# Attention scores two steps earlier in a twelve-step head loop, and another spread of the filling

## The chip, the cores and the metric

The kernel runs on one core of a Trainium2 chip. The core has five engines that run side by side, each through its own queue of instructions: TensorE (PE) multiplies matrices, VectorE (DVE) and ScalarE (ACT) work elementwise, GpSimd (POOL) and SyncE (SP) are used here almost only to issue DMA transfers. The metric is the time of one execution on the device in microseconds (us); lower is better. Before the change it is 2144.18 us, the median of 3 runs (2140.3 to 2147.97).

## The reference

One decoder layer in float32 on 512 tokens of width 2048: RMSNorm, a token mixer, a residual add, RMSNorm, a SwiGLU feed-forward network, a residual add, a final RMSNorm. The mixer is sparse attention with three branches; with 512 tokens the selected and the window branch both see every earlier token, so that each head has two causal softmaxes over 512 keys and one over 31 compressed keys:

```python
def masked_softmax(s, mask):
    s = jnp.where(mask, s.astype(jnp.float32), NEG_INF)
    p = jax.nn.softmax(s, axis=-1)
    return jnp.where(mask, p, 0.0)
...
s_c = jnp.einsum('btghd,bcgd->bghtc', q, kcc) + bias_c
p_c = masked_softmax(s_c, mask_c)
...
o = (gates[:, :, 0, :, :, None] * o_c + gates[:, :, 1, :, :, None] * o_s
     + gates[:, :, 2, :, :, None] * o_w)
return o.reshape(Bsz, S, N_HEADS * DH) @ w_out
```

There are 16 heads of width 128 in 4 groups; a group shares its keys and values. Queries, keys, values and gates are slices of one product of the normed input with `nsa_w_in`.

## The kernel before

**Three products for one.** Every float32 operand is split into a high part and a rest: ACT copies the value to the shorter format (`hi`), DVE subtracts (`lo`). `three` (L267 to L269) then multiplies hi by hi, hi by lo and lo by hi. For a weight block of 128x1024 that is one ACT copy `whi` (L97) and one DVE subtraction `wlo` (L98), in `Weights.split`. `Weights.take` hands out the next block and splits the one three places further on; `load` fetches raw blocks into three buffers.

**The stage that the change touches** lies between about 200 and 715 us of the span: the attention of the 16 heads, written out by hand in one order for all engines (`manual_schedule`). Each engine executes its share in the order of the program text. Two kinds of work are woven together:

- *The filling* (`dense`, L728): 13 projections of later heads (units `qpair`, `kpair`, `vpair`, 32 groups of matmuls each, four weight blocks each, so a block is taken at every eighth group) and then four `partial` products with `nsa_w_out` (24 groups, three blocks each). A group counts 650 in `done["ns"]`. At the end of a unit its result leaves PSUM (`q_out`, `k_out`: on DVE `yt`, L319, then on ACT `qh`, L292, then on DVE `ql`, L293).
- *A head* in twelve steps: `scores(h, t)` for the token tiles t = 3, 2, 1, 0 (PE writes the one PSUM tile `s`; DVE adds the bias and takes the row extreme, three L797 instructions into `cx` and `u`; ACT exponentiates, L799), `finish(h, t)` (DVE scales and transposes `p`, L804 to L812, and SP stores it to `d_p` in four DMAs, L814), `fetch(t)` (SP loads it back in the turned layout into `ptr`, L818, after the stores have landed), `turn(h, b, kt)` (ACT copies `pth`, L835, DVE subtracts `ptl`, L839) and `values(h, b, kt)` (PE multiplies into the tile `o`; L850 for the compressed branch, b = -1). `head_out` (L855) lets ACT copy `o` to `stage` and SP store it.

While head h is turned and multiplied, the scores of head h + 1 are made. In the loop of head h, `turn` number i stands at step i (0 to 8) and `values` two steps later; `scores(h + 1, t)` stand at steps 2, 5, 8, 11, `finish(h + 1, t)` at steps 3, 6, 9 and at step 0 of the next loop; `fetch(3)` and `fetch(2)` at step 8, `fetch(1)` and `fetch(0)` at steps 0 and 3 of the next loop. Ahead of loop 0 the scores of head 0 are made. Each step ends with `pump(h, step)`, which issues filling until `done["ns"]` has reached a goal four steps ahead of the step: 20800 (one unit) for a head, so 32 groups in twelve steps. A weight block is thus taken, and one split, at the ends of steps 0, 3, 6 and 7 in the loops 2 to 11 (at step 7 the end of a unit draws the last split forward). `drain_to` is a safeguard that issues filling until a needed unit is done.

In unit 13 (`qpair(14)`, the filling of loops 11 and 12) the buffers of the normed input are free piece by piece: `reload_o(i)` (POOL, 1 MB) brings the outputs of heads 4i to 4i + 3 back, and `split_o(k)` (L699 on ACT, L700 on DVE, 128x1024 each) splits two heads for the `partial` products.

Of the kernel before, what the change touches and what calls it, by code (L numbers as in the profile page):

```python
# [19 lines left out]
S, D, H, DH, G, HPG = 512, 2048, 16, 128, 4, 4  # L20
# [153 lines left out]
def nsa_block(ctx: ExitStack, tc: tile.TileContext, x, rel_bias, mix_g, ffn_g, fin_g, w_in, w_out,  # L174
# [30 lines left out]
    def tok(t):  # L205
        return slice(128 * t, 128 * (t + 1))
# [59 lines left out]
    def three(o, ah, al, bh, bl, start, stop):  # L266
        mm(o, ah, bh, start=start, stop=False, skip_group_check=True)  # L267
        mm(o, ah, bl, start=False, stop=False, skip_group_check=True)  # L268
        mm(o, al, bh, start=False, stop=stop, skip_group_check=True)  # L269

    def ws(ps, gi, g, c0=0, c1=S, start=None, end=None, of=None):

        for u in range(2):
            cs = slice(128 * u, 128 * (u + 1))
            if end and gi == 3 and u:
                W.ahead(3)
            for k in range(4):
                kk = 4 * gi + k
                st = (kk == 0) if start is None else (start and kk == 0)
                three(ps[u][:, c0:c1], g[0][:, k, cs], g[1][:, k, cs],  # L280
                      *(x[:, kk, c0:c1] for x in of or (hn_h, hn_l)), st, kk == KC - 1)
                if end and gi == 3 and k == 3:
                    end(u)
                yield 650
# [57 lines left out]
    def q_out(ps, h0):  # L342
        def end(u):
            Q[h0 + u] = tuple(qp.tile([128, S], F32R, name=f"q{n}") for n in "hl")
            split_from(normed(ps[u], SCALE), Q[h0 + u][0], Q[h0 + u][1])

        return end
# [282 lines left out]
    with ExitStack() as st2:  # L630
# [18 lines left out]
        def proj2():  # L649
            pool_ = (psx, ps2)[next(units) % 2]  # L650
            return [pool_.tile([128, 512], F32, name="proj") for _ in range(2)]

        def qpair(h0):
            ps = proj2()
            end = q_out(ps, h0)
            for i in range(4):
                yield from ws(ps, i, W.take(), end=end)
                if h0 == H - 2 and i < 3:
                    reload_o(i)
                if h0 == H - 2 and i > 1:  # L660
                    split_o(i - 2)
            done["n"] += 1
            yield None

# [29 lines left out]
        def reload_o(i):  # L694
            pool.dma_start(hn_l[:, 4 * i:4 * i + 4].bitcast(F32), d_o[i].rearrange("h p s -> p h s"))

        def split_o(k):
            h, l = (x[:, 2 * k:2 * k + 2] for x in (hn_h, hn_l))
            act(h, l.bitcast(F32), AF.Copy)  # L699
            dve.tensor_tensor(l, l.bitcast(F32), h.bitcast(F32), op=OP.subtract)  # L700
# [39 lines left out]
        STEPS = 12  # L740

        def pump(h, step):
            at = h + (step + 4) / STEPS
            goal = 20800 * min(at, 13) + 22500 * max(at - 13, 0)
            while done["ns"] < goal:
                c = next(stream, "end")
                if c == "end":
                    return
                done["ns"] += c or 0

        def drain_to(n):
            while done["n"] < n:
                c = next(stream, "end")
                if c == "end":
                    return
                done["ns"] += c or 0

        def needed(h):

            return 4 * ((h - 2) // 4) + (1 if h % 4 > 1 else 3) if h > 1 else 0  # L760
# [4 lines left out]
        def load_bias(h):  # L765
            if h < H:
                TB[h] = ap_.tile([128, S], F32, name="tb")
                (nc.sync if h else pool).dma_start(TB[h], bass.AP(tensor=d_u.tensor, offset=d_u.offset + h * UL + 127,
                                                 ap=[[H * UL - 1, 128], [1, S]]))

        def branch(t, b):

            return P[t][:, :, 32 * (t + 1) * b:32 * (t + 1) * (b + 1)]

        def scores(h, t):
            g, n = h // HPG, 128 * (t + 1)
            (qh, ql), (kh, kl) = Q[h], KK[g % 2]
            if t == NT - 1:
                HS[h] = dict(
                    mx=ap_.tile([128, NT, 3], F32, name="mx"), sm=ap_.tile([128, NT, 3], F32, name="sm"))  # L780
            s = HS[h]
            at = 224 + (512 if t == 1 else 0)
            cuts = [0, 288] + [c for c in (800, 1056) if c <= 32 + 2 * n]
            if cuts[-1] < 32 + 2 * n:
                cuts.append(32 + 2 * n)
            for c0, c1 in zip(cuts, cuts[1:]):
                three(sc[:, at + c0:at + c1], qh[:, tok(t)], ql[:, tok(t)], kh[:, c0:c1], kl[:, c0:c1], True, True)
            c = CX[t][:, :NCMP]
            regions = [(c, c, c, sc[:, at:at + NCMP], biasc[:, h, 24 - 8 * t:24 - 8 * t + NCMP])]
            bt = TB[h][:, S - n:].rearrange("p (n s) -> p n s", s=128)  # L790
            sw = sc[:, at + 32:at + 32 + 2 * n].rearrange("p (n b s) -> p b n s", b=2, s=128)
            for b in range(2):
                u = ap_.tile([128, S], F32, name="u")[:, :n]
                regions.append((u.rearrange("p (n s) -> p n s", s=128), u.rearrange("p (n j s) -> p j n s", j=4, s=32),
                                branch(t, b).rearrange("p j (n s) -> p j n s", s=32), sw[:, b], bt))
            for i, (u, v, p, ps, bias) in enumerate(regions):
                dve.tensor_tensor_reduce(out=u, in0=ps, in1=bias, op0=OP.add, op1=OP.min, scale=-1.0,  # L797
                                         scalar=1e38, accum_out=s["mx"][:, t, i:i + 1])
                act(p, v, AF.Exp, bias=s["mx"][:, t, i:i + 1], scale=-1.0, accum_out=s["sm"][:, t, i:i + 1])  # L799
            s[t] = [c] + [branch(t, b) for b in range(2)]  # L800

        def finish(h, t):
            r = HS[h]["sm"][:, t]
            dve.reciprocal(r, r)  # L804
            dve.tensor_mul(r, r, gates[:, t, h])
            for i, p in enumerate(HS[h].pop(t)):
                o = p
                if not i:
                    o = P[t][:, :3, runs[t] - 32:]
                    p = CX[t].unsqueeze(1).to_broadcast([128, 3, 32])  # L810
                dve.tensor_scalar(o, p, r[:, i:i + 1], None, op0=OP.mult)
            dve.transpose(P[t], P[t])  # L812
            for i in range(4):
                nc.sync.dma_start(d_p[t][:, :, i].rearrange("j a r -> a j r"), P[t][32 * i:32 * (i + 1)])  # L814

        def fetch(t):

            nc.sync.dma_start(PT[:, :, PT_STEP * t:PT_STEP * t + runs[t]], d_p[t].rearrange("j a i r -> (j a) i r"))  # L818
# [47 lines left out]
        load_bias(0)  # L866
        load_bias(1)
        for i in range(4):
            scores(0, 3 - i)
            if i > 1:  # L870
                fetch(5 - i)
            if i:
                finish(0, 4 - i)
            pump(-1, min(9 + i, 11.7))
        for h in range(H):
            seq = [(b, kt) for kt in (3, 2, 1, 0) for b in (0, 1)] + [(-1, 0)]
            for i in range(STEPS):
                if i == 4:
                    load_bias(h + 2)
                if i in (0, 3):  # L880
                    fetch(1 - i // 3)
                if i < 9:
                    turn(h, *seq[i])
                if i == 8 and h + 1 < H:
                    fetch(3)
                    fetch(2)
                if i == 0:
                    finish(h, 0)
                if h + 1 < H:
                    if i == 2:  # L890
                        drain_to(needed(h + 1))
                    if i % 3 == 2:
                        scores(h + 1, 3 - i // 3)
                    elif i % 3 == 0 and i:
                        finish(h + 1, 4 - i // 3)
                if 2 <= i < 10 or i == 11:
                    if i == 2 and h % HPG == 0:
                        drain_to(h)
                    values(h, *seq[min(i - 2, 8)])
                    if i == 11:  # L900
                        head_out(h)
                pump(h, i)
# [592 lines left out]
```

## Time and profile before

| | |
|---|---|
| median of 3 runs | 2144.18 us |
| the profiled execution | 2143.05 us, of which 2141.3 us are the span of the page |
| PE busy | 2105.8 us (98%), 14697 matmuls |
| DVE busy | 1634.8 us (76%) |
| ACT busy | 929.2 us (43%) |
| granted TensorE clock, mean | 0.993 |

The share of PE is counted with modelled ends: a matmul counts as busy until the next one can follow, so short waits hardly show. In rows of the timeline the columns are start, duration (both in us), engine, line, operation, result<-operands, shapes, and in brackets how long the engine had stood idle before and for whom. In rows of windows they are the stretch, its length, and for PE, PEld, DVE, ACT and POOL the busy time with the number of instructions, then the granted clock, the share of the DMA engines and GB/s.

### The profile page before, as it was taken

To read this page: it belongs to the slowest core of one execution; us is meant where nothing else is said; L and a number is where in the kernel's file an instruction comes from. 1 tells how busy PE (TensorE), PEld (TensorE's weight loads), DVE (VectorE), ACT (ScalarE), POOL (GpSimd) and SP (SyncE) were. 2 spreads that over 40 slices of the span, in tenths; PEclk is the share of its full clock that TensorE was granted. 3 is DMA by queue.
4 is the path that set the end of the run, shared out by engine and by line. 5 is a ranking of instruction groups with operands and counts; after the bars stand their busy time and mean duration, and the time that the engine had idled before them with its cause. 6 is when DMAs were issued, how large, how long until landed. Compare 5 with 4: busy or idle time off the path is not lost.

```text
span 2141.3 us, 37148 instructions
## 1 busy us (share of the span) xinstructions
PE 2105.8 (98%) x14697; PEld 1951.4 (91%) x14697; DVE 1634.8 (76%) x2674; ACT 929.2 (43%) x1439; POOL 128.0 (6%) x209
## 2 busy tenths in 40 slices
PE   9999999999979999999999999999999999999998
PEld 7898788898969889899999999999999888989996
DVE  5565777877767347898888888888888787877785
ACT  5344455555544234434434344344344444544344
POOL 1000111111101000000000000000000000001000
PEclk9999999999989999999999999999999999999999
DMA  7554666666757633344434344343443776878894
GB/s 232 179 148 147 186 197 197 183 197 188 217 179 233 221 127 128 109 137 130 127 120 126 122 129 129 119 128 119 129 128 126 253 277 217 295 272 309 307 331 151
DMA packets 271867, 388.08 MB, mean 181 GB/s; under 512 B 34523, under 2 KB 204555, under 8 KB 271052
## 3 DMA queue, kind: packets, MB, share of 16 engines
q1 hardware_dynamic: 245932, 275.52, 41.0%
q0 software_dynamic: 23856, 105.98, 14.2%
q10 hardware_dynamic: 1904, 4.20, 0.5%
q8 instruction: 115, 1.88, 0.4%
q14 instruction: 60, 0.49, 0.1%
HBM read 320.52 MB, written 70.36 MB: 183 GB/s over the span
## 4 chain that ended last, share of the span: by engine, by line
PE 67%; DMA 1%; DVE 1%; ACT 1%; issue 0%; SPq 0%; ACTq 0%; DVEq 0%
PE f L268 19%; PE f L269 19%; PE f L267 19%; PE proj L267 1%; PE proj L268 1%; PE proj L269 1%; PE pp L267 1%; PE pp L268 1%; PE pp L269 1%; PE po L268 1%; PE po L267 1%; PE po L269 1%; DMA tt<-d_a 0%; PE pp L245 0%; DMA d_p<-p 0%
## 5 line engine op out<-in xcount | busy, mean ns | idle before, releaser
L98 DVE TENSOR_TENSOR wlo<-raw,whi 128x1024 fp32r<-128x1024 f32 (+1 forms) x226 | 270.7, 1200 | 115.2 <-ACT whi L97 115.1
L97 ACT ACTIVATE whi<-raw 128x1024 fp32r<-128x1024 f32 (+1 forms) x226 | 234.4, 1040 | 223.2 <-DVE raw L994 121.7
L994 DVE TENSOR_TENSOR tlo<-tt,thi 128x1536 fp32r<-128x1536 f32 (+2 forms) x135 | 197.1, 1460 | 109.7 <-ACT thi L1096 88.8
L267 PE MATMUL f<-hn_h,whi 128*128 128x256 f32 x984 | 271.7, 276 | 0.8 <-ACT E L1054 0.8
L269 PE MATMUL f<-hn_h,wlo 128*128 128x256 f32 x984 | 271.6, 276 | 0.0
L268 PE MATMUL f<-hn_l,whi 128*128 128x256 f32 x984 | 271.6, 276 | 0.0
L1091 ACT ACTIVATE whi<-raw 128x1024 fp32r<-128x1024 f32 x123 | 126.1, 1057 | 292.2 <-DVE raw L994 282.0
L267 PE MATMUL proj<-hn_h,whi 128*128 128x512 f32 x512 | 205.4, 401 | 0.5 <-ACT hn_h L402 0.5
L268 PE MATMUL proj<-hn_l,whi 128*128 128x512 f32 x512 | 201.7, 394 | 0.3 <-DVE hn_l L403 0.3
L269 PE MATMUL proj<-hn_h,wlo 128*128 128x512 f32 x512 | 201.6, 394 | 0.0
L267 PEld LDWEIGHTS f<-hn_h,whi 128*128 128x128 f32 x984 | 184.7, 188 | 1.2 <-ACT E L1054 1.2
L269 PEld LDWEIGHTS f<-hn_h,wlo 128*128 128x128 f32 x984 | 184.7, 188 | 0.0
L268 PEld LDWEIGHTS f<-hn_l,whi 128*128 128x128 f32 x984 | 184.7, 188 | 0.0
L1096 ACT ACTIVATE thi<-tt 128x1536 fp32r<-128x1536 f32 x82 | 121.9, 1487 | 84.1 <-PE f L268 84.1
L267 PE MATMUL proj<-whi,hn_h 128*128 128x256 f32 (+2 forms) x496 | 146.6, 296 | 5.9 <-ACT hn_h L699 5.9
L269 PE MATMUL proj<-whi,hn_l 128*128 128x256 f32 (+2 forms) x496 | 146.0, 294 | 2.1 <-DVE hn_l L700 2.1
L994 DVE TENSOR_TENSOR wlo<-raw,whi 128x1024 fp32r<-128x1024 f32 x123 | 147.0, 1223 | 0.0
L268 PE MATMUL proj<-wlo,hn_h 128*128 128x256 f32 (+2 forms) x496 | 145.5, 293 | 0.0
L269 PE MATMUL f<-whi,tlo 128*128 128x512 f32 x320 | 124.9, 390 | 0.6 <-DVE tlo L994 0.6
L268 PE MATMUL f<-wlo,thi 128*128 128x512 f32 x320 | 125.0, 391 | 0.3 <-DVE wlo L98 0.3
L267 PE MATMUL f<-whi,thi 128*128 128x512 f32 x320 | 124.7, 390 | 0.0
L839 DVE TENSOR_TENSOR ptl<-ptr,pth 128x128 fp32r<-128x128 f32 (+3 forms) x128 | 60.0, 485 | 76.7 <-ACT pth L835 72.9
(327 smaller groups left out, 6142.6 us busy)
## 6 DMA issues: line engine op xcount, KB each, us to landing
raw<-in_ffn_w_in SPq DMA_DIRECT2D x135, 512.0 KB, 3.6
raw<-in_ffn_w_out SPq DMA_DIRECT2D x88, 512.0 KB, 5.9
rawx<-in_ffn_w_in SPq DMA_DIRECT2D x41, 512.0 KB, 4.9
rawx<-d_a SPq DMA_DIRECT2D x31, 512.0 KB, 4.9
ah<-d_s POOLq DMA_DIRECT2D x16, 896.0 KB, 7.4
al<-d_s POOLq DMA_DIRECT2D x16, 896.0 KB, 10.1
raw<-in_nsa_w_in SPq DMA_DIRECT2D x24, 512.0 KB, 4.6
raw<-in_nsa_w_in POOLq DMA_DIRECT2D x24, 512.0 KB, 4.4
```

The lines of the kernel that those rows point to most:

```text
L97: self.nc.scalar.activation(hi[:, :n], src, AF.Copy)
L98: self.nc.vector.tensor_tensor(lo[:, :n], src, hi[:, :n].bitcast(F32), op=OP.subtract)
L267: mm(o, ah, bh, start=start, stop=False, skip_group_check=True)
L268: mm(o, ah, bl, start=False, stop=False, skip_group_check=True)
L269: mm(o, al, bh, start=False, stop=stop, skip_group_check=True)
L839: dve.tensor_tensor(tl4, src, th4.bitcast(F32), op=OP.subtract)
L994: dve.tensor_tensor(o, a, b, op=OP.subtract)
L1091: act(h, r, AF.Copy)
L1096: act(h, ttf, AF.Copy)
```

## The change

Four things are moved; no arithmetic is added or taken away.

1. `scores(h + 1, t)` stand at steps 0, 3, 6, 9 and `finish(h + 1, t)` at steps 1, 4, 7, 10: two steps earlier, counted in steps of the loop. `fetch(1)` stands at step 9 and `fetch(0)` at step 0 of the next loop, three steps earlier; `fetch(3)` and `fetch(2)` stay at step 8.
2. `pump` aims 4 + (4 - 2 at) steps ahead while `at`, the place in heads, is below 2: about nine steps ahead of loop 0, eight at its start, six at the start of loop 1, four from loop 2 on. The filling ahead of loop 0 is put before each of its scores, not after.
3. The last tile of head 0 is finished ahead of loop 0.
4. In `qpair(14)` each `reload_o` comes one quarter of the unit later, and `split_o(0)` and `split_o(1)` stand together at its end.

```diff
@@ qpair
-                if h0 == H - 2 and i < 3:
-                    reload_o(i)
-                if h0 == H - 2 and i > 1:
-                    split_o(i - 2)
+                if h0 == H - 2 and i:
+                    reload_o(i - 1)
+                    if i == 3:
+                        split_o(0)
+                        split_o(1)
@@ pump
-            at = h + (step + 4) / STEPS
+            at = h + step / STEPS
+            at += (4 + max(4 - 2 * at, 0)) / STEPS
@@ ahead of the loop of heads
         for i in range(4):
+            pump(-1, 5 + 2 * i)
             scores(0, 3 - i)
             if i > 1:
                 fetch(5 - i)
             if i:
                 finish(0, 4 - i)
-            pump(-1, min(9 + i, 11.7))
+        pump(-1, 11.7)
+        fetch(1)
+        finish(0, 0)
@@ the loop of heads
-                if i in (0, 3):
-                    fetch(1 - i // 3)
+                if i == 0:
+                    fetch(0)
                 if i < 9:
                     turn(h, *seq[i])
-                if i == 8 and h + 1 < H:
+                if i == 8 and more:
                     fetch(3)
                     fetch(2)
-                if i == 0:
-                    finish(h, 0)
-                if h + 1 < H:
-                    if i == 2:
+                if i == 9 and more:
+                    fetch(1)
+                if more:
+                    if i == 0:
                         drain_to(needed(h + 1))
-                    if i % 3 == 2:
+                    if i % 3 == 0:
                         scores(h + 1, 3 - i // 3)
-                    elif i % 3 == 0 and i:
-                        finish(h + 1, 4 - i // 3)
+                    elif i % 3 == 1:
+                        finish(h + 1, 3 - i // 3)
```

`more` is `h + 1 < H`. The order in which each engine gets its instructions follows from the text. In the loops 2 to 11 (one with a q unit as the example) DVE goes:

```
before: scores3, ptl, finish3, wlo, ptl, ptl, scores2, ptl, finish2, wlo, ptl, yt, ql, wlo, pth, scores1, yt, ql, finish1, scores0, ptl, finish0, wlo, ptl, ptl
after:  scores3, wlo, ptl, finish3, ptl, ptl, scores2, wlo, ptl, finish2, ptl, ptl, scores1, wlo, ptl, finish1, yt, ql, wlo, pth, yt, ql, scores0, finish0, ptl
```

(`scores3` is short for the three L797 instructions of t = 3, `finish3` for L804 to L812, `pth` for the subtraction of the compressed branch.) ACT has the matching copies and exponentials in the same order.

More of the change, by code (lines that the diff above doesn't have):

```diff
@@ L877, in nsa_block @@
             for i in range(STEPS):
+                more = h + 1 < H
                 if i == 4:
                     load_bias(h + 2)
-                if i in (0, 3):
-                    fetch(1 - i // 3)
+                if i == 0:
+                    fetch(0)
                 if i < 9:
                     turn(h, *seq[i])
-                if i == 8 and h + 1 < H:
+                if i == 8 and more:
                     fetch(3)
                     fetch(2)
-                if i == 0:
-                    finish(h, 0)
-                if h + 1 < H:
-                    if i == 2:
+                if i == 9 and more:
+                    fetch(1)
+                if more:
+                    if i == 0:
                         drain_to(needed(h + 1))
-                    if i % 3 == 2:
+                    if i % 3 == 0:
                         scores(h + 1, 3 - i // 3)
-                    elif i % 3 == 0 and i:
-                        finish(h + 1, 4 - i // 3)
+                    elif i % 3 == 1:
+                        finish(h + 1, 3 - i // 3)
                 if 2 <= i < 10 or i == 11:
```

## The prediction

> **What bounds the kernel now.** I first cut the heads' stage into windows: the start with loop 0, two steady loops, the place where the outputs are reloaded, the end.
>
> ```profile
> 201.78:254.73 52.95, 47.09 (x212) 38.77 (x212) 36.85 (x112) 22.82 (x67) 4.50 (x6) 0.94 0.60 171
> 494.33:524.19 29.86, 29.86 (x146) 25.06 (x145) 23.46 (x67) 15.44 (x43) 4.48 (x6) 1.00 0.70 198
> 524.19:554.06 29.87, 29.87 (x188) 26.88 (x187) 23.47 (x66) 15.22 (x41) 4.47 (x6) 1.00 0.68 196
> 594.00:626.00 32.00, 19.42 (x83) 16.04 (x82) 18.76 (x40) 12.60 (x25) 2.99 (x4) 0.73 0.66 202
> 706.00:713.00 7.00, 5.27 (x26) 3.36 (x25) 4.86 (x7) 1.67 (x3) 1.47 (x2) 1.00 0.34 108
> ```
>
> PE is idle for 5.9 us at the start (52.95 - 47.09), 12.6 us around 610 and 1.7 us at the end; the clock is lower in the first two. That is what the change can win. In the steady loops PE shows no idle time in 29.86 us, and DVE is busy for 23.5 us, which looks like six spare microseconds. The timeline of a steady loop says otherwise. Here are DVE, ACT, PE and SP in one order of time (one loop and the beginning of the next):
>
> ```profile
> 535.32 0.18 DVE L797 CUSTOM_DVE_ANT_0 cx<-s,biasc 128x31 f32<-128x31 f32 x1
> 537.24 0.62 ACT L835 ACTIVATE pth<-ptr 128x512 fp32r<-128x512 f32 x1
> 537.88 0.69 DVE L839 TENSOR_TENSOR ptl<-ptr,pth 128x512 fp32r<-128x512 f32 x1 [1.42 <-ACT pth L835]
> ...
> 543.86 1.05 ACT L97 ACTIVATE whi<-raw 128x1024 fp32r<-128x1024 f32 x1
> 544.94 1.23 DVE L98 TENSOR_TENSOR wlo<-raw,whi 128x1024 fp32r<-128x1024 f32 x1 [0.26 <-ACT whi L97]
> 546.20 0.68 DVE L837 TENSOR_TENSOR pth<-ptr,pth 32x512 fp32r<-32x512 f32 x1
> 546.91 0.19 DVE L797 CUSTOM_DVE_ANT_0 cx<-s,biasc 128x31 f32<-128x31 f32 x1
> 546.91 1.22 SPq L818 DMA_DIRECT2D ptr<-d_p  x2
> 547.71 0.69 DVE L319 SCALAR_TENSOR_TENSOR yt<-proj,ybc 128x512 f32<-128x512 f32 x1
> 547.85 0.40 PE L267 MATMUL s<-k0h,qh 128*128 128x288 f32 x1
> 548.49 0.62 ACT L292 ACTIVATE qh<-yt 128x512 fp32r<-128x512 f32 x1
> 549.14 0.69 DVE L293 TENSOR_TENSOR ql<-yt,qh 128x512 fp32r<-128x512 f32 x1 [0.74 <-ACT qh L292]
> ...
> 551.76 0.15 DVE L797 CUSTOM_DVE_ANT_0 cx<-s,biasc 128x31 f32<-128x31 f32 x1
> 553.05 0.58 ACT L859 ACTIVATE stage<-o 128x512 f32<-128x512 f32 x1
> 553.85 0.29 DVE L839 TENSOR_TENSOR ptl<-ptr,pth 128x128 fp32r<-128x128 f32 x1 [1.51 <-ACT pth L835]
> 554.06 0.17 DVE L804 RECIPROCAL sm<-sm 128x3 f32<-128x3 f32 x1
> 555.68 1.19 DVE L98 TENSOR_TENSOR wlo<-raw,whi 128x1024 fp32r<-128x1024 f32 x1
> ...
> 557.32 0.18 DVE L797 CUSTOM_DVE_ANT_0 cx<-s,biasc 128x31 f32<-128x31 f32 x1
> 559.59 0.40 ACT L835 ACTIVATE pth<-ptr 128x256 fp32r<-128x256 f32 x1
> 560.02 0.42 DVE L839 TENSOR_TENSOR ptl<-ptr,pth 128x256 fp32r<-128x256 f32 x1 [1.28 <-ACT pth L835]
> ...
> 563.17 1.18 DVE L98 TENSOR_TENSOR wlo<-raw,whi 128x1024 fp32r<-128x1024 f32 x1
> 564.27 0.55 DVE L839 TENSOR_TENSOR ptl<-ptr,pth 128x384 fp32r<-128x384 f32 x1
> ```
>
> Every gap of DVE here ends with ACT (1.42, 0.26, 0.74, 1.51, 1.28), none with PE or a DMA. And PE starts `scores0` at 547.85, just after DVE has read `scores1` out of the tile `s` (until about 547.79): a small wait of PE on DVE that the busy share hides. So DVE and ACT, passing work to and fro in their fixed orders, set the pace of 29.86 us, and PE runs at almost the same pace behind. **An added wait in that exchange is paid in every loop**; taking PE's work elsewhere wins nothing there.
>
> **The steady loops (2 to 11), part by part.** No instruction is added; what counts is which DVE instruction follows each `scores`. Weight splits still fall at steps 0, 3, 6 and 7, but now `scores` stand at 0, 3, 6, so `wlo` comes straight behind the three L797, and its `whi` stands on ACT behind the exponentials. From the start of `scores` to the next DVE instruction:
>
> - t = 3: before 2.70 (557.32 to 560.02). After: ACT is through with the exponentials 2.27 later (559.59), and `wlo` follows the start of `whi` by 1.08 (543.86 to 544.94): 3.35.
> - t = 2: before 2.56 (535.32 to 537.88); after 1.92 (537.24) + 1.08 = 3.00.
> - t = 1: before 0.80 (546.91 to 547.71, `yt` needs no ACT); after 1.58 (548.49) + 1.08 = 2.66.
> - t = 0: before 2.09 (551.76 to 553.85); after, `finish0` follows, which needs the last exponential: 1.29 (553.05) + 0.13, an estimate for reading its sum: 1.42.
> - `wlo` itself takes 1.10 to the next start when it had not to wait (563.17 to 564.27) and 1.26 when it had (544.94 to 546.20): three of them, + 0.48.
>
> Sum: (3.35 + 3.00 + 2.66 + 1.42 + 0.48) - (2.70 + 2.56 + 0.80 + 2.09) = 10.91 - 8.15 = **+2.76 us per loop**.
>
> [...]
>
> A second wait comes up. `fetch(3)` can only start once DVE's `pth` has read `ptr` (546.20 + 0.68, and SP issues at 546.91). The next `turn` of t = 3 needs it:
>
> ```profile
> ptr<-d_p SPq DMA_DIRECT2D x16, 576.0 KB, 5.7
> ```
>
> Landing 5.7 us after issue, then ACT's copy (0.3): about 6.05 from the end of `pth` to `ptl`. Before, DVE had 6.97 us of other work there (546.88 to 553.85), so nobody waited. After, `finish1` has left that stretch: `yt` to `ql` 1.4, `ql` 0.6, `scores0` to `finish0` 1.42, `finish0` 1.62 (554.06 to 555.68) make 5.05. The transfer is late by 1.0; bounds 0 (it lands in 5.0) and 2 (behind it now two more fetches share the queue). I take 0.85, below the median row, since some landed sooner than it. Together **+3.6 us per loop**, bounds 2.7 and 4.8, for ten loops: +36 (27 to 48). PE then stands idle for about 3.6 us per loop, in pieces: behind `pth` for `values` of the compressed branch, and behind `scores0` for the next `scores3`.
>
> **The start and loops 0 and 1.** Marks are the first L797 of `scores3`:
>
> ```profile
> 205.34 0.19 DVE L797 CUSTOM_DVE_ANT_0 cx<-s,biasc 128x31 f32<-128x31 f32 x1 [0.58 <-PE s L269]
> ...
> 221.66 0.51 ACT L835 ACTIVATE pth<-ptr 128x128 fp32r<-128x128 f32 x2 [3.77 <-DMA ptr<-d_p]
> ...
> 228.03 0.18 DVE L797 CUSTOM_DVE_ANT_0 cx<-s,biasc 128x31 f32<-128x31 f32 x1
> ...
> 287.85 0.18 DVE L797 CUSTOM_DVE_ANT_0 cx<-s,biasc 128x31 f32<-128x31 f32 x1
> ...
> 587.13 0.18 DVE L797 CUSTOM_DVE_ANT_0 cx<-s,biasc 128x31 f32<-128x31 f32 x1
> ```
>
> From the first mark of head 0 to its first turned tile pass 16.3 us (205.34 to 221.66), a chain through DVE, store and fetch that filling cannot shorten. The six groups now in front (18 matmuls at 29.86/146 us are 3.7 us) replace an idle PE but set the mark to about 207; one split more stands in the chain (+2). The first `ptl` comes near 225.5, and head 1's mark near 226, against 228.03: 2 us won (bounds -3 and +5). Loop 0 stays at about 29.9. In loop 1 the splits fall at steps 1, 4, 6 and 11, so only t = 1 pays (+1.86 + 0.16, and -0.67 at t = 0), and the fetch has less work over it (1.42 + 1.62 + 1.1 against 6.05): +1.9, about 33.1. Head 3's mark: 226 + 29.9 + 33.1 = 289 against 287.85, **+1**. The extra filling ahead buys PE time, but DVE sets these loops too.
>
> Head 13's mark: before 587.13. After 289 + 10 x (29.86 + 3.6) = 623.6: **+36.5**.
>
> **The reload (loop 12).** Two stalls sit here now:
>
> ```profile
> PE proj L267 <- ACT hn_h L699: 5.9, 1, 5.9
> ...
> 597.54 0.69 PE L267 MATMUL o<-pth,v1h 128*128 128x384 f32 x1 [2.62 <-ACT pth L835]
> 598.00:600.00 2.00, 2.00 (x6) 1.68 (x6) 1.61 (x8) 1.25 (x5) 0.00 (x0) 0.50 0.90 254
> ...
> 604.00:606.00 2.00, 2.00 (x10) 1.64 (x10) 0.93 (x3) 1.63 (x3) 0.00 (x0) 1.00 0.30 111
> ...
> 617.29 2.93 ACT L699 ACTIVATE hn_h<-hn_l 128x1024 fp32r<-128x1024 f32 x3
> 621.28 0.58 PE L269 MATMUL proj<-whi,hn_l 128*128 128x256 f32 x1 [2.10 <-DVE hn_l L700]
> ```
>
> The first, a `fetch(1)` late behind the reload, goes away with three more steps. But the first `partial` needs `split_o(0)` and `split_o(1)`, and these now stand together behind `scores0` on DVE and ACT. Counted from a mark, DVE ended `pth` at 19.4 (546.88, the mark being one loop before 557.32). After, two more `ptl` (0.55), one more `wlo` (1.1), `scores1` (2.66), `finish1` (2.0, from the end of `ql` to 551.76) and the added waits (0.65 + 0.44 + 0.48) come ahead of it: 27.3. `yt` and `ql` follow (2.0), so `scores0` at 29.4; its exponentials end at 30.7, and the two splits on ACT and DVE (1.08, then 1.2 each) at 34.1. Before, the same matmul came at 621.28, also 34.1 behind the mark (587.13). So the stall of `values` is traded for a longer one: **0** (bounds -6 and +4; the later third reload is due two steps after its issue, covered by eight groups).
>
> **The end.** `fetch(0)` and `finish(15, 0)` come earlier, so the 1.7 us idle near 709 go: **-1.7** (bounds -1.7, 0). In loops 13 to 15 `yt` and `ql` are gone from DVE and PE sets the pace; 0.
>
> **Sum:** on the profiled execution's 2143.05 us (1.1 below the median shown): + 36.5 + 0 - 1.7 = 2177.8; with that 1.1 half counted, **2178**.
>
> **The rivals.**
> 1. *DVE has room, and only the stalls change* (the other side). PE at 98% and no idle in ten loops speak for it; the wait at 547.85 and DVE's gaps, all on ACT, against. Then: start -5.9 and some 2 for the clock, the late fetch -2.6 and 3 for the half clock behind it, end -1.7: about 2129. It decides if the added cost per loop is under 1 us. Chance 0.10.
> 2. *The fetch lands in time*: 2.76 per loop, loop 1 shorter by 1.8: 2178 - 8.5 - 1.9 = 2168. Chance 0.20.
> 3. *PE's new gaps drop the clock in every loop.* A gap of 2.62 was followed by clock 0.50; mine are near 1.6 and 1.0, close together. At half clock for some 6.5 us (597.54 to 604) PE loses 3.2 us per loop, nearly its new idle time; if 1.2 spills over, 2178 + 12 = 2190. Chance 0.10. [...]
> 4. *Something small*: gains and costs cancel within 6 us. Chance 0.02.
>
> **How the numbers follow.** The forecast has 0.58. A difference under 0.3% (6.4 us) can't be told from none. Faster: rival 1, 0.10. Same: 0.02. Slower: the forecast and rivals 2 and 3, 0.88. Range: from 2158 (rival 2 with a start 10 us better placed) to 2192 (rival 3); it leaves rival 1 out, and some of the tails.
>
> **What would show it.** Right: `wlo` behind ACT `whi` waits of 1.9 us three times a loop, marks of `scores3` 33.5 us apart, some 3.6 us of idle PE per loop, ACT waiting for `ptr`, no idle near 597, a wait of `proj` on L699 that is longer than 5.9. Wrong: marks still 29.9 apart, or PE without idle time between 260 and 560.

## The result, and the profile after

The changed kernel is slower: 2173.76 us (median of 4 runs, 2171.39 to 2175.54) against 2144.3 us (4 runs), ratio 1.0137 with a 95% interval of 1.0116 to 1.0158. The profiled execution took 2171.39 us, its span is 2169.6 us (before 2141.3) and its mean clock 0.996. The code lines have moved a little: L797, L799, L835, L837, L839, L859 of before are now L799, L801, L837, L839, L841, L861, and L699 and L700 are L700 and L701.

The windows of the changed kernel, at the places that were shown of before: the start with loop 0, one steady loop, the loop with the reload (from the mark of head 13 to that of head 14), the end.

```profile
201.78:253.55 51.77, 46.15 (x212) 37.29 (x211) 37.30 (x111) 22.96 (x66) 4.51 (x6) 0.97 0.55 158
...
549.62:582.97 33.35, 30.90 (x169) 26.34 (x169) 23.84 (x65) 15.58 (x43) 4.78 (x6) 1.00 0.62 176
619.37:662.34 42.97, 31.64 (x171) 27.14 (x170) 31.33 (x74) 21.08 (x46) 6.38 (x9) 0.88 0.71 225
735.00:742.00 7.00, 6.76 (x47) 5.62 (x45) 4.88 (x8) 1.85 (x4) 1.47 (x2) 1.00 0.47 160
```

A steady loop now takes 33.35 us, and PE, which showed no idle time there, is idle for 2.45 us of it at full clock. The end lost most of its idle time (0.24 us in seven, before 1.73). Here is DVE in the timeline, with the marks of heads 1, 3 and 13 and, between them, one steady loop (one row is ACT's, where it waits for the fetched tile):

```profile
225.57 0.18 DVE L799 CUSTOM_DVE_ANT_0 cx<-s,biasc 128x31 f32<-128x31 f32 x1
...
288.43 0.18 DVE L799 CUSTOM_DVE_ANT_0 cx<-s,biasc 128x31 f32<-128x31 f32 x1
...
552.72 0.31 ACT L837 ACTIVATE pth<-ptr 128x128 fp32r<-128x128 f32 x1 [1.64 <-DMA ptr<-d_p]
553.07 0.29 DVE L841 TENSOR_TENSOR ptl<-ptr,pth 128x128 fp32r<-128x128 f32 x1 [0.97 <-ACT pth L837]
553.28 0.18 DVE L799 CUSTOM_DVE_ANT_0 cx<-s,biasc 128x31 f32<-128x31 f32 x1
...
556.62 1.23 DVE L98 TENSOR_TENSOR wlo<-raw,whi 128x1024 fp32r<-128x1024 f32 x1 [1.93 <-ACT whi L97]
557.76 0.28 DVE L841 TENSOR_TENSOR ptl<-ptr,pth 128x128 fp32r<-128x128 f32 x1
...
561.58 0.18 DVE L799 CUSTOM_DVE_ANT_0 cx<-s,biasc 128x31 f32<-128x31 f32 x1
...
564.58 1.23 DVE L98 TENSOR_TENSOR wlo<-raw,whi 128x1024 fp32r<-128x1024 f32 x1 [1.85 <-ACT whi L97]
...
569.63 0.18 DVE L799 CUSTOM_DVE_ANT_0 cx<-s,biasc 128x31 f32<-128x31 f32 x1
...
572.28 1.23 DVE L98 TENSOR_TENSOR wlo<-raw,whi 128x1024 fp32r<-128x1024 f32 x1 [1.77 <-ACT whi L97]
...
582.31 0.18 DVE L799 CUSTOM_DVE_ANT_0 cx<-s,biasc 128x31 f32<-128x31 f32 x1
...
583.75 0.17 DVE L806 RECIPROCAL sm<-sm 128x3 f32<-128x3 f32 x1 [0.83 <-ACT p L801]
...
619.37 0.18 DVE L799 CUSTOM_DVE_ANT_0 cx<-s,biasc 128x31 f32<-128x31 f32 x1
```

And ACT in the same view, behind the `cx` of 553.28:

```profile
554.84 0.71 ACT L801 ACTIVATE p<-u,mx 128x512 f32<-128x512 f32 x1
...
555.54 1.04 ACT L97 ACTIVATE whi<-raw 128x1024 fp32r<-128x1024 f32 x1
```

The `whi` of the split starts only when the last exponential is done (555.54), and DVE, whose next instruction is `wlo`, stands still until 556.62. It happens behind three of the four `scores`, with waits of 1.93, 1.85 and 1.77 us in the rows above. The view of waits adds up who stood still for whom. For DVE in the kernel before, over two whole loops from mark to mark (497.56 to 557.32; the columns are the total in us, how often, the longest):

```profile
DVE ptl L839 <- ACT pth L835: 8.4, 6, 1.5
DVE ql L293 <- ACT qh L292: 1.4, 2, 0.7
DVE k1l L293 <- ACT k1h L292: 1.4, 2, 0.7
DVE wlo L98 <- ACT whi L97: 0.5, 2, 0.3
```

The same in the changed kernel (519.64 to 586.74), where `ql` and `k1l` are as before:

```profile
DVE wlo L98 <- ACT whi L97: 11.6, 8, 1.9
DVE ptl L841 <- ACT pth L837: 3.1, 3, 1.1
DVE sm L806 <- ACT p L801: 1.7, 2, 0.8
...
```

The two loops grew by 7.34 us, from 59.76 to 67.10. A list also takes in a wait that ends just ahead of its stretch: of the three of `ptl` one (1.02 us, in front of the `ptl` of 519.43) belongs to the loop ahead, so two loops have 2.1. DVE's waits grew by 11.1 for `wlo` and 1.7 for `sm`, and shrank by 6.3 for `ptl`: 6.5 in sum, and its busy time grew by 1.0. The time is found; whether this exchange is its cause, the experiments had to show.

### The profile page after: what moved, and what is told of

The parts are those of the page before. It is cut to its first block, busy times and chain, and to the rows that moved or that the text cites. A ratio compares the mean times of both kernels' runs of the same rounds, so it can differ in the third digit from the quotient of the medians.

```text
span 2169.6 us, 37138 instructions
## 1 busy us (share of the span) xinstructions
PE 2110.7 (97%) x14697; PEld 1947.6 (90%) x14697; DVE 1640.7 (76%) x2674; ACT 931.9 (43%) x1439; POOL 129.7 (6%) x209
## 4 chain that ended last, share of the span: by engine, by line
PE 71%; DVE 7%; ACT 4%; issue 3%; DMA 3%; DVEq 0%; ACTq 0%; SPq 0%
PE f L269 19%; PE f L268 19%; PE f L267 19%; PE proj L267 2%; PE proj L269 2%; PE proj L268 2%; DMA ptr<-d_p 2%; ACT whi L97 2%; DVE ptl L841 2%; DVE p L813 2%; DVE wlo L98 1%; ACT p L801 1%; PE pp L267 1%; PE pp L269 1%; PE pp L268 1%
## 5 line engine op out<-in xcount | busy, mean ns | idle before, releaser
L269 PEld LDWEIGHTS proj<-hn_h,wlo 128*128 128x128 f32 x512 | 96.4, 188 | 21.6 <-DVE wlo L98 0.2
```

## The experiments

All ratios are against the kernel before, measured alongside.

| run | what it is | us | ratio, 95% interval |
|---|---|---|---|
| lead5_after | changed kernel, filling five steps ahead | 2135.28 | 0.9957 (0.9942 to 0.9972) |
| own_t3_after | changed kernel, a tile of its own for t = 3 | 2160.34 | 1.0075 (1.0058 to 1.0092) |
| lead5_t3_after | both | 2131.59 | 0.9941 (0.9926 to 0.9956) |
| filling_alone | before, with part 2 | 2146.95 | 1.0016 (1.0006 to 1.0025) |
| scores_alone | changed kernel without part 2 | 2174.96 | 1.0148 (1.0133 to 1.0164) |
| lead5_before | before, filling five steps ahead | 2189.85 | 1.0222 (1.0204 to 1.0239) |
| dve_added | before, 0.84 us more DVE work a loop | 2154.57 | 1.0056 (1.0041 to 1.0071) |
| lead5_dve_added | lead5_after, the same added | 2138.35 | 0.9978 (0.9968 to 0.9987) |
| reload_alone | before, with part 4 | 2134.51 | 0.9960 (0.9946 to 0.9974) |
| reload_undone | changed kernel without part 4 | 2173.61 | 1.0147 (1.0132 to 1.0162) |
| lead5_t3_reload | lead5_t3_after, splits of the reload earlier | 2131.19 | 0.9946 (0.9931 to 0.9961) |
| filling_first | changed kernel, filling ahead of scores in a step | 2171.95 | 1.0128 (1.0107 to 1.0149) |

### Who sets the pace

The prediction stood on DVE and ACT setting the 29.86 us although PE shows no idle time. That can be asked directly: two more additions for DVE in every loop, on a tile that nothing else reads.

```diff
+        spare = ap_.tile([128, 256], F32, name="spare", bufs=1)
+        pool.memset(spare, 0.0)
...
+                if i == 8:
+                    dve.tensor_tensor(spare, spare, spare, op=OP.add)
+                    dve.tensor_tensor(spare, spare, spare, op=OP.add)
```

> The kernel before with two more DVE additions of 128x256 (0.42 us each by the group L839) in every loop, just ahead of the cx of scores1. Theory (DVE and ACT set the 29.86 us of a steady loop): all of the 0.84 us is paid, ten loops and more, 2151 to 2154. Rival (PE sets the pace, and the exchange of DVE and ACT has some slack): less than 0.3 us per loop, at most 2147.

Measured: 12.0 us more, just above the range, and steady loops of 30.68 us, 0.80 longer. Of 0.84 us of added DVE work nearly all is paid, so DVE was on the path. PE, which in two loops of the kernel before (497.56 to 557.32) has no row in the list of waits, now has one (504.04 to 565.55):

```profile
PE s L267 <- DVE mx L799: 1.6, 2, 0.8
```

The same edit in the changed kernel with lead 5 (below):

> The changed kernel with lead 5 and two more DVE additions of 128x256 in every loop ahead of the cx of scores0. The same 0.84 us cost the kernel before 12 us. Theory (with the splits away from the scores, DVE has slack and PE sets the loops of 29.8 us): at most 0.3 us per loop, 2134 to 2139. Rival (DVE and ACT still set the pace, only at a shorter length): 2144 to 2148.

Measured: 2138.35 against 2135.28 us, 3.1 more. From mark 3 to mark 13 it is 0.19 us per loop, so most of the work is hidden, as the theory had it. But the list of DVE's waits over two loops (498.75 to 558.63) shows where:

```profile
DVE ptl L843 <- ACT pth L839: 5.0, 4, 1.3
...
```

Without the additions the row has 6.3 us and seven waits (below). Gone are the waits for the fetched tile, 0.48 us per loop on average from mark 3 to mark 13: the additions stand between the start of the fetch and this wait and take its place. So this run does not show by itself that PE sets the pace there.

### Where the splits fall

One number in `pump` moves all filling one step ahead, and with it the splits, from steps 0, 3, 6, 7 to 2, 5, 6, 11. `scores` stand at 0, 3, 6, 9 in the changed kernel.

```diff
-            at += (4 + max(4 - 2 * at, 0)) / STEPS
+            at += (5 + max(4 - 2 * at, 0)) / STEPS
```

> The changed kernel with the filling's lead raised by one step (4 to 5) and nothing else. The weight splits of a steady loop then fall at steps 2, 5, 6 and 11, so none but one stands straight behind scores. Theory (the cost is wlo waiting for a whi that is queued behind the exponentials on ACT): the three waits of about 1.9 us go, the loops of heads 2 to 11 take about 31.5 us (30.6 plus the wait for the late fetch) in place of 33.4, and the time falls by some 19 to about 2155. Rival (the earlier place of the scores costs by itself, wherever the splits stand): 2174, loops still at 33.4.

The direction was right, the size was not: 2135.28 us, 38 below the changed kernel instead of 19, and below the kernel before. DVE's waits over two loops (497.21 to 556.53; one of the seven of `ptl`, 0.51, belongs to the loop ahead):

```profile
DVE ptl L841 <- ACT pth L837: 6.3, 7, 1.3
DVE sm L806 <- ACT p L801: 1.7, 2, 0.8
...
DVE wlo L98 <- ACT whi L97: 0.5, 2, 0.3
```

The three waits for `whi` are gone, as expected, and two loops take 59.32 us. The timeline shows what had not been counted:

```profile
526.75 0.29 DVE L841 TENSOR_TENSOR ptl<-ptr,pth 128x128 fp32r<-128x128 f32 x1 [0.37 <-ACT pth L837]
...
529.55 0.29 DVE L841 TENSOR_TENSOR ptl<-ptr,pth 128x128 fp32r<-128x128 f32 x1 [1.18 <-ACT pth L837]
...
542.32 0.42 DVE L799 CUSTOM_DVE_ANT_0 u<-s,tb 128x256 f32<-128x256 f32 x1
542.66 0.68 DVE L319 SCALAR_TENSOR_TENSOR yt<-proj,ybc 128x512 f32<-128x512 f32 x1
```

With the filling, `yt` moved too, and now stands straight behind `scores1`. It needs nothing of ACT, so DVE does not wait there at all. The fetched tile costs 0.37 us in place of 0.97, and behind `scores3` stands a `ptl` that waits 1.18 instead of a `wlo` that waits 1.9.

The second suspected cost, the late `fetch(3)`, was taken away alone, by a small tile for the columns that the first two turns read, fetched at step 4 of the loop before:

```diff
+        P3 = ap_.tile([128, 2, 4, 32], F32, name="ptr3", bufs=1)
...
+                nc.sync.dma_start(P3[:, b], d_p[3][..., c:c + 32].rearrange("j a i r -> (j a) i r"))
...
+            elif kt == 3:
+                src = P3[:, b:b + 1]
```

> The changed kernel with a small tile of its own for the part of the last tile (t = 3) that the first two turns of a head read; it is fetched at step 4 of the loop before, long ahead. Theory (the fetch behind the compressed pth is late by about 1 us in every loop): the gap of about 1 us before ptl of the first turn goes, loops of 32.4 us in place of 33.4, about 2165. Rival (the fetch is hidden, ptl would wait there for something else, as long): 2174, loops unchanged.

Measured: 2160.34 us, 13.4 less than the changed kernel. Two loops (511.48 to 576.32) take 64.84 us, 1.13 less for each, and the row for `ptl` and `pth` is gone from the list, the row for `wlo` unchanged:

```profile
DVE wlo L98 <- ACT whi L97: 11.6, 8, 1.9
DVE sm L807 <- ACT p L802: 1.7, 2, 0.8
...
```

So the fetch was late, and 32.42 - 29.88 = 2.54 us per loop are left for the splits. Both edits together:

> Both edits together: lead 5 and the t = 3 tile of its own. Theory (the two waits are the whole of the added cost and they add up): loops of about 30.6 us, some 28 less in all, about 2147. Rival (taking one wait away only uncovers the other, or PE's order is the cost): not below the better one of the two alone by more than 3 us.

Measured: 2131.59 us, only 3.7 below lead 5 alone, though far below what was expected. The two costs don't add up any more. DVE's waits for the fetched tile, 4.8 us in the ten loops from mark 3 to mark 13, are gone, but these loops only shrink from 298.19 to 296.46 us. A floor has been reached. In the list of DVE's waits over two loops (494 to 553.46) there is a new row:

```profile
DVE cx L800 <- PE s L269: 0.3, 1, 0.3
```

And the window of the same two loops:

```profile
494.00:553.46 59.46, 59.46 (x325) 51.72 (x324) 47.74 (x130) 30.84 (x82) 9.03 (x13) 1.00 0.72 200
```

Here DVE waits for PE's scores, which it did in none of the other lists of steady loops, and PE is never idle. The busy share alone would not prove much, since it showed no idle time in the kernel before either. The start times do: 512 columns take PE 0.23 us from one start to the next, and in `lead5_t3_reload` (below), where the same ten loops also take 296.46 us, no matmul of them starts more than 0.06 us later than the columns of the one ahead of it ask for at that rate. PE runs without a pause, so it sets these loops, at 29.73 us in the two shown (59.46 / 2), 0.15 below the pace of before.

### The scores and the filling, each alone

The changed kernel with the old filling:

```diff
-            at = h + step / STEPS
-            at += (4 + max(4 - 2 * at, 0)) / STEPS
+            at = h + (step + 4) / STEPS
...
         for i in range(4):
-            pump(-1, 5 + 2 * i)
             scores(0, 3 - i)
...
-        pump(-1, 11.7)
+            pump(-1, min(9 + i, 11.7))
```

> The changed kernel with the filling of before (four steps ahead throughout, four calls in front of loop 0): scores, finishes, fetches and the reload as changed. The splits of the steady loops stand as in the changed kernel. Theory: steady loops at 33.4 us, loop 2 now too, time 2172 to 2182. Rival (the larger lead at the first heads is part of the cost): below 2165.

Measured 2174.96 us with steady loops between 32.8 and 34.8: the whole loss, without part 2. Part 2 alone, in the kernel before:

```diff
-            at = h + (step + 4) / STEPS
+            at = h + step / STEPS
+            at += (4 + max(4 - 2 * at, 0)) / STEPS
...
         for i in range(4):
+            pump(-1, 5 + 2 * i)
             scores(0, 3 - i)
...
-            pump(-1, min(9 + i, 11.7))
```

> The kernel before with the new filling alone: eight to ten steps ahead at head 0, spread between its scores, falling to four at head 2; scores, finishes and the reload stay where they were. Theory (DVE and ACT set the loops, and filling ahead buys only PE time): steady loops stay at 29.9 us, and head 3's first mark stays within 4 us of 287.85; time 2140 to 2148. Rival (the filling itself is what costs the time): above 2155.

Measured 2146.95 us, steady loops of 29.9, head 3's mark at 291.33, 3.5 behind that of before. The larger lead at the first heads wins nothing by itself; it costs these 3.5 us.

### The order within the step, and a lead of five without the earlier scores

If `wlo` behind the exponentials were all, it should be enough to exchange `scores` and the filling within a step:

```diff
                     if i % 3 == 0:
+                        pump(h, i)
                         scores(h + 1, 3 - i // 3)
...
-                pump(h, i)
+                if i % 3 or not more:
+                    pump(h, i)
```

> The changed kernel, lead 4, with the call of the filling in steps 0, 3, 6 and 9 put ahead of scores in place of behind it; nothing else. The splits keep their steps, and stand ahead of the scores of the same step in the programs of DVE and ACT. Theory (it is only the order within the step, whi behind the exponentials on ACT, that costs the time): most of the 3.4 us per loop goes, loops of 29.8 to 31, 2134 to 2146. Rival (three splits so near the scores crowd DVE and ACT in whichever order, or the filling behind scores is needed on PE while DVE reads them): above 2160.

The rival's number came true: 2171.95 us. DVE's waits over two loops (521.04 to 586.65, 65.61 us):

```profile
DVE ptl L841 <- ACT pth L837: 9.9, 8, 1.3
DVE wlo L98 <- ACT whi L97: 2.5, 5, 0.7
DVE sm L806 <- ACT p L801: 1.7, 2, 0.8
...
```

The waits of `wlo` fell from 11.6 to 1.8 (the fifth of the list, 0.66, belongs to the loop ahead), but those of `ptl` rose from 2.1 to 9.9. What stands behind `scores` on DVE and needs ACT inherits the wait in these runs: here a `ptl` behind each of three `scores` (1.18, 1.31 and 1.34 us), and DVE reads the scores later, since `wlo` now comes ahead of `cx`. Lead 5 wins because `scores1` has `yt` behind it and because the splits stand a step away: all of DVE's listed waits sum to 16.9 us in these two loops and to 10.8 in the two with lead 5, and the loops differ by about as much (65.61 against 59.32).

The mirror image is the kernel before with lead 5, where the splits of steps 2, 5 and 11 come straight behind its `scores`:

```diff
-            at = h + (step + 4) / STEPS
+            at = h + (step + 5) / STEPS
```

> The kernel before with the filling's lead raised from 4 to 5 steps, scores where they were. The splits then fall at steps 2, 5, 6 and 11, and scores stand at 2, 5, 8 and 11: three splits come straight behind scores, as in the changed kernel. Theory (a split straight behind scores costs its wlo a wait for whi behind the exponentials; the changed kernel with a t = 3 tile of its own showed 2.4 us per loop for three of them): loops of 31.5 to 32.3 us in place of 29.9, time 2160 to 2168. Rival (the cost belongs to the earlier scores): loops unchanged, 2144.

Measured: 2189.85 us. The theory's direction holds and the rival falls (no scores were moved), but the loops take 34.0 us, more than expected. DVE's waits over two loops (501.4 to 569.32):

```profile
DVE wlo L98 <- ACT whi L97: 12.6, 8, 2.3
DVE ptl L839 <- issue: 3.3, 3, 1.2
...
```

PE in the timeline of one of them:

```profile
518.43 0.39 PE L269 MATMUL proj<-hn_h,wlo 128*128 128x512 f32 x1
519.99 0.50 PE L267 MATMUL o<-pth,v0h 128*128 128x512 f32 x1 [1.17 <-ACT pth L835]
521.34 0.50 PE L268 MATMUL o<-ptl,v0h 128*128 128x512 f32 x1 [0.84 <-DVE ptl L839]
...
523.53 0.63 PE L269 MATMUL proj<-hn_h,wlo 128*128 128x512 f32 x1
```

And the windows there (the clock is the third number from the end):

```profile
518.00:522.00 4.00, 1.99 (x8) 1.12 (x7) 3.12 (x4) 2.02 (x4) 0.75 (x1) 1.00 0.48 116
522.00:526.00 4.00, 4.00 (x12) 3.13 (x11) 2.51 (x10) 2.51 (x8) 0.00 (x0) 0.57 0.56 158
```

The waits of `wlo` are as large as in the changed kernel (12.6 against 11.6). What comes on top is a lower clock (0.95 over these two loops, 1.00 over the two of the kernel before): 0.57 over four microseconds is 1.7 us of PE's work (4 x 0.43), and 2.4 + 1.7 would be the 4.1 by which the loop grew. The row with `issue`, where the profile names no cause, fits it: the `ptl` of 534.90 starts 0.09 us after PE has ended the `o<-ptl` of 534.53 (0.28 long), which reads the buffer that this `ptl` overwrites. (One of the three waits belongs to the loop ahead.) DVE, it seems, waits there for a PE that has fallen behind. That the sum is the cause was not tried by itself.

### The reload

Part 4 alone, in the kernel before (the edit of `qpair` as the change has it):

```diff
-                if h0 == H - 2 and i < 3:
-                    reload_o(i)
-                if h0 == H - 2 and i > 1:
-                    split_o(i - 2)
+                if h0 == H - 2 and i:
+                    reload_o(i - 1)
+                    if i == 3:
+                        split_o(0)
+                        split_o(1)
```

> The kernel before with the change at the reload alone: the three reloads each one group later, split_o(0) and split_o(1) both behind the last group. Theory (the late fetch in loop 12 shares its queues with the reload, and the second stall comes from the order of the splits on ACT and DVE): the stall of 2.62 us near 597 may shrink, the wait of proj for L699 of 5.9 stays or grows; 2140 to 2146. Rival (the five us that the changed kernel gains between the marks of heads 13 and 15 come from this part): 2139 or less.

Measured: 2134.51 us, 8.1 less; the rival's number was right (its cause was not, as the next run shows). The window from mark 13 to mark 14 in the kernel before:

```profile
587.13:635.27 48.14, 35.56 (x192) 30.98 (x191) 31.18 (x73) 21.01 (x46) 5.92 (x8) 0.82 0.60 188
```

And in this kernel:

```profile
586.41:627.61 41.20, 32.89 (x192) 29.66 (x191) 31.07 (x73) 20.79 (x46) 6.67 (x9) 0.88 0.76 236
```

6.9 us of it lie here: PE's idle time falls from 12.6 to 8.3, the late fetch is gone, the clock over the window is 0.88 in place of 0.82, and the wait of `proj` for `hn_h` stays (6.2). In the changed kernel the same part can be taken out again, by the same diff read backwards:

> The changed kernel with the reload as it was before: reloads behind groups 0, 1 and 2, split_o(0) behind group 2 and split_o(1) behind group 3. Theory (the part is worth the same 8 us here as alone): 2179 to 2184, with a stall of values behind a late fetch near 630 again. Rival (by the prediction's sum, the reload comes out even in the changed kernel, since the fetch goes earlier anyway): 2171 to 2176.

Measured: 2173.61 against 2173.76 us. There the part is worth nothing, as the rival had it: its fetches go earlier in any case, and the first stall doesn't come back, against what the theory expected. Last, the splits of the reload put ahead of the last `yt`, in the best kernel so far:

```diff
-                if h0 == H - 2 and i:
-                    reload_o(i - 1)
-                    if i == 3:
+                if h0 == H - 2:
+                    if i != 2:
+                        reload_o(min(i, 2))
+                    else:
                         split_o(0)
                         split_o(1)
```

> Lead 5 and the t = 3 tile of its own, and the reloads behind groups 0, 1 and 3 with split_o(0) and split_o(1) behind group 2, ahead of the last yt. Theory (the wait of 5.9 us of proj for hn_h comes from the two splits standing behind scores and yt on ACT and DVE): that wait falls under 2 us, the clock stays up there, 2122 to 2128 against 2131.6 without it. Rival (PE then waits for the next thing there, or the fetch is late again): 2130 to 2134.

Measured: 2131.19 against 2131.59 us, no difference. PE's waits from 575 to 740:

```profile
PE proj L269 <- DVE hn_l L703: 2.3, 3, 0.8
PE proj L267 <- ACT hn_h L702: 2.0, 2, 1.3
...
```

The one wait of 5.9 us became five short ones, probably because the next splits are now the late ones, and the clock falls all the same (0.67 from 615 to 619). The loop is 2.2 us shorter (37.31 against 39.47), but an early loop came out 1.2 longer (30.21 against 29.03), which was not traced.

## Why the prediction was right, point by point

**The forecast** of 2178 us was 4.2 above the median; its main mechanism was right, and its largest term was too large.

**The pace.** That time added to DVE's order is paid nearly in full, in spite of a PE without idle time, is shown by `dve_added`. With the 3.3 us by which the loops grew it also settles the first rival (DVE has room). PE's own pace lies only 0.15 below. Of the forecast 3.6 us of idle PE per loop the windows show 2.6 ((67.10 - 61.82) / 2), because PE counts as busy up to its modelled ends; the places are those forecast.

**The steady loops.** The four stretches from `scores` to the next DVE instruction came out as worked out: 3.34, 3.00, 2.65 and 1.44 us in the timeline above (forecast 3.35, 3.00, 2.66, 1.42). The term for `wlo` itself was too large: 1.14 us to the next start where 1.26 was taken, so 0.12 per loop and not 0.48. (The row of 1.26 had `pth` behind it, and there the changed kernel also has 1.26; the wait had nothing to do with it.) That makes 2.40 instead of 2.76, and `own_t3_after` has 2.54. The late fetch was too small: 1.13 by the same run (DVE's waits in front of that `ptl` average 0.92 over the ten loops), 0.85 forecast. The errors cancel by luck: 3.6 forecast, 3.67 in the two loops shown. The second rival (the fetch in time) is refuted by the same run.

What failed is the count "for ten loops". From mark 3 to mark 13 the changed kernel takes 330.94 us, before 299.28: 31.7 more, not 36. In loop 2 the filling that ran ahead is still being caught up, only two splits stand behind `scores`, and it takes 31.35 us (33.43 in `scores_alone`, where nothing runs ahead). That is 2.1 of the 4.3; the other nine are 33.29 on average (33.46 forecast, 1.5 in sum), and one loop of 30.55 in the kernel before makes the rest.

**The start.** Head 1's mark is at 225.57 (forecast 226), head 3's at 288.43 (289). But loop 0 took 31.5 (29.9) and loop 1 31.4 (33.1): in loop 0 one split does come behind `scores0`, in loop 1 the fetch was late by 0.5 only. Two misses that cancel, by luck again.

**The reload.** "Traded for a longer one: 0" had the stalls right and the sum wrong. No stall near 597 is left, and the wait for `hn_h` grew:

```profile
PE proj L267 <- ACT hn_h L700: 9.8, 1, 9.8
```

PE's idle time from mark 13 to mark 14 is 11.3 us against 12.6. But there is only one stretch of low clock (0.50 to 0.53 in windows of half a microsecond from 645.87 to 655.87), not two (in the kernel before 0.50 from 597.13 to 603.63 and from 614.63 to 624.13). In 5.5 us of the one stretch PE was idle, so an estimate multiplies, in each of these windows, PE's busy time with what the granted clock lacks: 2.2 us are lost where 5.2 were. Together 4.2 of the 5.2 us by which this loop is shorter. The sum had counted the stalls and left the clock behind them out. `reload_undone` shows that most of this gain is the earlier fetch's, not the edit's: the loop takes 43.84 us without the edit, 42.97 with it.

**The end.** Between the mark of head 13 (+32.2 us) and the end of the span (+28.3) 3.9 us come back, 1.7 forecast. The idle time at the end went nearly as forecast (1.5) and the loop of the reload gave 5.2; that is 2.8 too much, and where these are lost again was not traced.

**The third rival**, a clock that drops in every loop, did not occur in the changed kernel (1.00 in the steady windows) but did in both loops looked at of `lead5_before` (0.57 from 522 to 526 in the one), with one matmul between two gaps and not seven.

**What the prediction did not see** is that its cost is no property of the earlier scores. Its words "what counts is which DVE instruction follows each `scores`" were right, yet it took the places of the splits as given. One step more of lead makes the same order of scores 8 us faster than the kernel before, not 30 slower.

## What to carry to other kernels

Where two engines pass work to and fro in fixed orders, look at what stands directly behind each hand-over. In this case an instruction that needed the other engine waited for what stood ahead there (`wlo` 1.8 to 1.9 us behind the exponentials), and one that needed nothing of it (`yt`) did not wait. When a scheduler's lead or step is changed, list that successor for every hand-over before and after; it decided 38 us here, while PE's busy share moved from 97% to 99% and DVE's from 76% to 77%. And the worth of an edit depends on what else is on the path: the same reload edit won 8 us in one kernel and none in the other, and a fix of 13 us alone was worth 4 behind another.

## What the runs showed of the hardware

In `lead5_before` idle times of PE of 1.17 and 0.84 us, with a single matmul between them (519.99 to 521.34), were followed by a lower clock: 0.75, 0.50, 0.50 and 0.55 in the four microseconds from 522 to 526, with matmuls of 0.63 us in place of 0.39, and 1.00 again behind them. In the other loop looked at, idle times of 1.41 and 0.85 us were followed by matmuls of 0.63 us too. In the changed kernel waits of 1.48 and 0.75 us, with seven matmuls in a row between them, left the clock at 1.00. PE in its timeline:

```profile
546.98 0.50 PE L852 MATMUL o<-pth,vcc 96*128 96x512 f32 x1 [1.48 <-DVE pth L839]
...
549.62 0.40 PE L267 MATMUL s<-k0h,qh 128*128 128x288 f32 x1 [0.75 <-DVE mx L799]
```

And the windows behind the first:

```profile
547.00:551.00 4.00, 3.25 (x15) 2.46 (x16) 2.39 (x11) 2.46 (x10) 1.10 (x2) 1.00 0.72 194
551.00:555.00 4.00, 4.00 (x20) 3.34 (x20) 2.68 (x11) 1.69 (x7) 0.00 (x0) 1.00 1.11 319
```

So it is not the longest single gap that went with the low clock here. In `lead5_before` PE was idle for 2.0 us within 2.5 (518.82 to 521.34), in the changed kernel for 2.2 us spread over 4.1 (545.50 to 549.62). Why the clock fell in the one and not in the other was not shown.
